# Keys and values of the first cross attention made at the program's start and kept in DRAM

## The chip, the core and the metric

The kernel runs on one of the eight cores of a Trainium2 chip. The core has a TensorE (PE in the profile; its weight loads are PEld), a VectorE (DVE), a ScalarE (ACT), a GpSimd (POOL) and a SyncE (SP), each with its own instruction queue, and 16 DMA engines that move data between DRAM and the on-chip buffer. The metric is the device time of one execution in microseconds (us); smaller is better.

## The reference, cut to what matters

Two stacks of layers work on 256 tokens of 1024 features, one after the other. The first stack modulates its norms with a condition vector; its first mixer starts from a modulated norm of the input x. The second stack has two layers, each with a mixer, a cross attention over a fixed memory, and an MLP. Of the cross attention of its layer l (a summary of the reference, not its text):

```
m  = rmsnorm(memory, lnmem[l])                  # 256 x 1024, depends on an input alone
k  = headwise_rmsnorm(m @ xk[l], xkn[l])        # 4 heads of 256
v  = m @ xv[l]
q  = headwise_rmsnorm(rmsnorm(x, lnx[l]) @ xq[l], xqn[l])
x += softmax(q @ k.T / 16) @ v @ xo[l]
mod = silu(cond) @ Wmod + b                     # shift, scale and gate of the first stack
```

Nothing in k and v depends on the first stack: they need only the memory and the weights xk and xv.

## The kernel before, in words

The hidden state is kept transposed on chip, as `xT` of 128 partitions x 8 x 256. All weights stream from DRAM in blocks of 128x1024 float32 (512 KB), issued on SP's queue by `_dma` (L461) into four buffers `wraw`, up to three blocks ahead. Most blocks are then split into a rounded high part `wh` on ACT (L470) and the rest `wl` on DVE (L471), four buffers, two blocks ahead. A product is three matmuls (high x high, high x low, low x high), so a block takes 24 matmuls of 128x256, or 12 of 128x512. A few blocks are used raw: those of the modulation, and the first of the first mixer (`hy_ba`, the first `hy_qkv`).

The order of the blocks is the order in which the program asks for them (`block`). `together` takes turns between generators, one step each; `piped` keeps some units of a stream in flight; `late` starts a generator some turns later. The Tile framework then orders the instructions on each engine and adds the waits.

The start, in `mix` (L849): a `drain` (L891) runs four things side by side. `mod_part` (L726) takes 8 blocks `mod` on DVE, one multiply-and-sum over the block each (L730). `mod_rows` (L745) takes 8 blocks `modk` on PE into `ps_mr`, copies the rows to `mod_row`, and turns them into columns by `ps_mc`; with them `modT` is made. `steps` loads `xT` and sums its squares (`nsq`, `n_sum`). `spectrum` makes a filter for the second stack (`ps_f`, `ps_h`, `ps_abs`, `ps_rb`, and later its transform `ps_F`, with the constant tables `dftu` and `nyq`). Then `modulated` (L893) makes the first mixer's input `h_w` out of `xT`, the row factors `ps_rs` and `modT`, and the first matmuls of the mixer, `ps_g<-h_w,wraw`, follow. On a timeline these matmuls mark the end of the start.

The first cross attention: at the end of the second stack's first mixer (`mixb`, L1675) `memory` (L2146) loads the memory (`c_mem`, ACT's queue) and makes its scaled high and low parts `c_mh`, `c_ml` and its row sums beside the mixer's out projection (`ps_o`). `cross` (L2164) then takes 8 blocks `xv` (`unit_v`, L2210: `ps_v`, into `c_v`), 8 blocks `xk` (`unit`, L2184: `ps_g<-c_mh`, into `c_k`, with squares `c_sq`, their sums `ps_n`, and the norm factor `rf_f` spread over the partitions by `ps_rs`) and 8 blocks `xq` on the state (`ps_g<-hh`, into `c_q`), four units in flight. The attention (`ps_s<-c_k,c_q`) follows. `row_factor` is a chain of small DVE operations (`rf_u`, `is_i`, `is_a`, `rf_f`); the norm of a whole row has a like chain (`is_v` to `is_i`).

## Time and profile before

| what | value |
|---|---|
| time, median of 3 runs | 3307.97 us (3306.54 to 3317.33) |
| profiled execution, its own time | 3313.57 us |
| its span, first to last instruction | 3311.8 us |
| PE busy | 3239.4 us (98%) |
| DVE busy | 2526.4 us (76%) |
| ACT busy | 1599.8 us (48%) |
| mean granted TensorE clock | 0.992 of full speed |

The profiled execution took 1.8 us beside its span, and stands 5.6 us above the median. Busy is the time in which an engine has an instruction in work; PE's matmuls overlap one another, so the step from one start to the next is shorter than the length of a row.

### The profile page before, as it was taken

Reading aid. Unit: us, or ns where it says so; the run is one execution under the profiler, and the core shown is the slowest. Engines: PE = TensorE matmul, PEld = TensorE weight load, DVE = VectorE, ACT = ScalarE, POOL = GpSimd, SP = SyncE. Lnnn points to the kernel's source line nnn. Section 1 sums busy time; section 2 is a strip of 40 time slices with the busy share of each in tenths; the row PEclk is TensorE's granted clock in tenths of the full one; section 3 lists DMA queues with packets and bytes.
Section 4 is the critical chain, followed back from the end, with each engine's and each line's share of the span. In section 5 each row is a group of like instructions: output and inputs, shape, how many; then the busy total and the mean of one; then the engine's idle time right before and its main releaser. Section 6 shows DMA issues by size and latency. Waiting matters only on the chain.

```text
span 3311.8 us, 58824 instructions
## 1 busy us (share of the span) xinstructions
PE 3239.4 (98%) x23096; PEld 2870.1 (87%) x23096; DVE 2526.4 (76%) x5214; ACT 1599.8 (48%) x2530; POOL 11.3 (0%) x24
## 2 busy tenths in 40 slices
PE   7999999999999999999999999999999999999999
PEld 3889999998777769999898788879999987899998
DVE  6878999967977778999856955877766568767655
ACT  4435444444345545444444355555555454545544
POOL 0000000000000000000000000000000000000000
PEclk9999999999999999999999999999999999999999
DMA  7454555687478435655565466525456653545464
GB/s 250 143 184 139 179 180 172 201 276 255 147 251 278 146 103 154 185 184 159 173 185 174 145 192 189 179 87 156 143 164 197 185 158 98 148 138 179 132 188 140
DMA packets 158094, 574.45 MB, mean 173 GB/s; under 512 B 18346, under 2 KB 20077, under 8 KB 157049
## 3 DMA queue, kind: packets, MB, share of 16 engines
q1 hardware_dynamic: 152400, 551.99, 54.4%
q10 hardware_dynamic: 3816, 13.46, 1.1%
q0 software_dynamic: 1600, 5.24, 0.4%
q8 instruction: 181, 2.97, 0.4%
q14 instruction: 97, 0.79, 0.1%
HBM read 564.34 MB, written 6.29 MB: 172 GB/s over the span
## 4 chain that ended last, share of the span: by engine, by line
PE 60%; issue 33%; DVE 5%; ACT 1%; DMA 1%; POOL 0%; SPq 0%; ACTq 0%; POOLq 0%; DVEq 0%
PE ps_g L508 18%; PE acc L508 16%; PE ps_u L508 10%; PE ps_o L508 3%; PE ps_y L508 3%; PE ps_v L508 2%; DVE wl L471 1%; PE ps_s L508 1%; PE ps_po L508 1%; PE ps_F L508 1%; DVE p L520 1%; PE ps_G L508 1%; PE ps_go L508 1%; DMA wraw<-modk 0%; PE ps_pt L533 0%
## 5 line engine op out<-in xcount | busy, mean ns | idle before, releaser
L470 ACT ACTIVATE wh<-wraw 128x1024 fp32r<-128x1024 f32 x932 | 986.8, 1059 | 979.2 <-PE ps_u L508 358.7
L471 DVE TENSOR_TENSOR wl<-wraw,wh 128x1024 fp32r<-128x1024 f32 x932 | 1134.6, 1220 | 336.9 <-ACT wh L470 334.1
L508 PE MATMUL ps_u<-hh,wh 128*128 128x256 f32 x2048 | 580.3, 283 | 0.0
L508 PE MATMUL ps_u<-hh,wl 128*128 128x256 f32 x2048 | 577.5, 282 | 0.0
L508 PE MATMUL ps_u<-hl,wh 128*128 128x256 f32 x2048 | 575.4, 281 | 0.0
L508 PE MATMUL ps_g<-hh,wh 128*128 128x256 f32 (+1 forms) x1920 | 557.9, 292 | 7.5 <-ACT hh L517 4.0
L508 PE MATMUL ps_g<-hl,wh 128*128 128x256 f32 (+1 forms) x1920 | 547.0, 286 | 1.5 <-DVE hl L529 1.5
L508 PE MATMUL ps_g<-hh,wl 128*128 128x256 f32 (+1 forms) x1920 | 547.1, 286 | 0.0
L508 PEld LDWEIGHTS ps_g<-hh,wh 128*128 128x128 f32 x1920 | 367.1, 192 | 23.6 <-issue 6.0
L508 PEld LDWEIGHTS ps_u<-hl,wh 128*128 128x128 f32 x2048 | 387.0, 189 | 0.2
L508 PEld LDWEIGHTS ps_u<-hh,wl 128*128 128x128 f32 x2048 | 387.0, 189 | 0.0
L508 PEld LDWEIGHTS ps_u<-hh,wh 128*128 128x128 f32 x2048 | 385.9, 188 | 0.2
L508 PEld LDWEIGHTS ps_g<-hl,wh 128*128 128x128 f32 x1920 | 369.0, 193 | 7.5 <-issue 2.4
L508 PEld LDWEIGHTS ps_g<-hh,wl 128*128 128x128 f32 x1920 | 369.2, 193 | 0.9 <-issue 0.7
L508 PE MATMUL acc<-wh,pl 128*128 128x512 f32 x976 | 310.8, 398 | 2.9 <-DVE pl L520 2.8
L508 PE MATMUL acc<-wh,ph 128*128 128x512 f32 x976 | 312.8, 400 | 0.0
L508 PE MATMUL acc<-wl,ph 128*128 128x512 f32 x976 | 310.1, 397 | 0.0
L517 ACT ACTIVATE ph<-A 128x256 fp32r<-128x256 f32 x244 | 101.5, 417 | 323.0 <-PE acc L508 167.3
L508 PEld LDWEIGHTS acc<-wh,pl 128*128 128x128 f32 x976 | 181.9, 188 | 50.1 <-DVE pl L520 8.3
L508 PEld LDWEIGHTS acc<-wl,ph 128*128 128x128 f32 x976 | 183.4, 188 | 43.0
L508 PEld LDWEIGHTS acc<-wh,ph 128*128 128x128 f32 x976 | 181.0, 188 | 41.9 <-issue 1.4
L730 DVE SCALAR_TENSOR_TENSOR wraw<-wraw,cond 128x1024 f32<-128x1024 f32 x88 | 107.2, 1221 | 73.1 <-DMA wraw<-mod 72.8
(570 smaller groups left out, 4841.3 us busy)
## 6 DMA issues: line engine op xcount, KB each, us to landing
wraw<-u SPq DMA_DIRECT2D x256, 512.0 KB
wraw<-v SPq DMA_DIRECT2D x256, 512.0 KB
wraw<-w SPq DMA_DIRECT2D x128, 512.0 KB
wraw<-mod SPq DMA_DIRECT2D x88, 512.0 KB
wraw<-b_gate SPq DMA_DIRECT2D x48, 512.0 KB
wraw<-pq SPq DMA_DIRECT2D x32, 512.0 KB
wraw<-b_hy SPq DMA_DIRECT2D x24, 512.0 KB
wraw<-b_gla SPq DMA_DIRECT2D x18, 512.0 KB
```

The lines of the kernel that those rows point to most:

```text
L470: self.nc.scalar.activation(h, raw, AF.Copy)
L471: self.nc.vector.tensor_tensor(l, raw, h.bitcast(F), op=OP.subtract)
L508: self.nc.tensor.matmul(out, lhsT, rhs, start=start, stop=stop, skip_group_check=skip)
L517: self.nc.scalar.activation(out, in_, func, bias=bias, scale=scale, **k)
L520: self.nc.vector.tensor_tensor(out, a, b, op=op)
L730: self.nc.vector.scalar_tensor_tensor(w, w, 0.5, self.cond, op0=OP.mult, op1=OP.mult, accum_out=self.modT[l][:, j:j + 1])
```

## The change

In `mix`, before the mixer's own buffers are taken, `memory` is now called for the first cross attention. Its norm, the 8 `xv` blocks and the 8 `xk` blocks (`memory_units`, four units in flight) run inside the opening `drain`, taking turns with the modulation's weights; the spectrum starts four turns later. When keys and values are ready they are stored, 1 MB each, by GpSimd's DMA queue into a DRAM buffer `kv`. At the end of `mixb` the two are loaded back on ACT's queue in place of the memory and its norm, and `cross` of the first layer takes only its 8 `xq` blocks before the attention. The second layer's cross attention still makes its keys and values itself, by the same helper, in which `unit_v` now hands on after each block. The buffers of the first mixer are allocated after those of the new work are released.

```diff
             ectx = ExitStack()
             eps_ = ectx.enter_context(tc.tile_pool(name="earlyps", bufs=1, space=PSUM, reuse_waits="tile"))
...
+            def steps():
+                yield
+                for k in range(0, KT, 4):
+                    self.nc.scalar.dma_start(self.xT[:, k:k + 4], self.ap["xT"][:, k:k + 4])
+                yield
...
+            with ExitStack() as before:
+                ahead = iter(())
+                if "cross0" in self.stages:
+                    self.memory(0, before)
+                    (mem, nm), self.mem = self.mem, None
+                    kvp = before.enter_context(tc.tile_pool(name="memkv", bufs=1, reuse_waits="tile"))
+                    k = kvp.tile([P, KT, T], F, name="c_k")
+                    vt = kvp.tile([P, 2, D], F, name="c_v")
+                    self.kv = tc.dram_tile([P, 2, KT, T], F, name="kv")
+
+                    def prepared():
+                        for i in range(2, KT, 2):
+                            nm.step(i)
+                            nm.step(i + 1)
+                            yield
+                        yield from nm.tail()
+
+                    def stored():
+                        nm.step(0)
+                        nm.step(1)
+                        yield from together(prepared(), piped(self.memory_units(0, kvp, mem, nm, k, vt), 4))
+                        self.nc.gpsimd.dma_start(self.kv[:, 0], k)
+                        self.nc.gpsimd.dma_start(self.kv[:, 1], vt.rearrange("p t (a n) -> p (t a) n", n=T))
+
+                    ahead = stored()
+                first = before.enter_context(tc.tile_pool(name="first", bufs=1, reuse_waits="tile"))
+                self.cond_columns(first)
+                next(spectrum, None)
+                drain(together(ahead, self.mod_rows(0, 0, 8, first, eps_), self.mod_part(0, 8, 16), steps(),
+                               late(4, some(6, spectrum))))
             pool = ctx.enter_context(tc.tile_pool(name="hyb", bufs=1, reuse_waits="tile"))
...
-            drain(together(self.mod_part(0, 8, 16), self.mod_rows(0, 0, 8, early, eps_), steps(), some(6, spectrum)))
             self.load_constants()
             self.modulated(nrm, 0, 0, hw)
...
-                prepare = self.memory(l, self.memctx)
+                if l == 0 and self.kv is not None:
+                    kvp = self.memctx.enter_context(tc.tile_pool(name="memkv2", bufs=1, side="right", reuse_waits="tile"))
+                    k = kvp.tile([P, KT, T], F, name="c_k")
+                    vt = kvp.tile([P, 2, D], F, name="c_v")
+                    nc.scalar.dma_start(k, self.kv[:, 0])
+                    nc.scalar.dma_start(vt.rearrange("p t (a n) -> p (t a) n", n=T), self.kv[:, 1])
+                    self.mem = (k, vt, None)
+                else:
+                    prepare = self.memory(l, self.memctx)
             drain(together(self.project_out(f"b_out{l}", mh, ml), prepare))
...
+    def memory_units(self, l, pool, m, nm, k, vt):
+        def unit_v(b):
+            outs = [self.ps.tile([P, 512], F, name="ps_v", tag="mm") for _ in range(2)]
+            for i in range(4):
+                w = self.block(f"xv{l}", b * 4 + i)
+                self.gemm_o1(outs, w, m, 2, 2 * i, i == 0, i == 3)
+                yield
+            while nm.r is None:
+                yield
+            for t in range(2):
+                self.act(vt[:, t, b * 512:(b + 1) * 512], outs[t], AF.Copy, scale=nm.r[:, t:t + 1])
+            yield
+        for b in range(2):
+            yield unit_v(b)
+        for i in range(4):
+            yield self.cross_unit(pool, f"xk{l}", i, m, k, f"xkn{l}", nm)
...
+            def projections():
+                if len(held) == 2:
+                    yield from self.memory_units(l, pool, *held, k, vt)
                 for i in range(4):
-                    yield unit(f"xq{l}", i, (self.hh, self.hl), q, f"xqn{l}", nrm)
+                    yield self.cross_unit(pool, f"xq{l}", i, (self.hh, self.hl), q, f"xqn{l}", nrm, made)
```

Three places show how the instructions stand. First, SP's queue from its first weight block on, before the change; `mod0` and `modk0` are the modulation's blocks for DVE and for PE.

```order
L461 DMA wraw_134<-mod0 128x1024
L461 DMA wraw_136<-modk0 128x1024
L461 DMA wraw_138<-mod0 128x1024
L461 DMA wraw_140<-modk0 128x1024
L461 DMA wraw_142<-mod0 128x1024
L461 DMA wraw_144<-modk0 128x1024
```

The same queue from the same place on, with the change; `xv0` and `xk0` are the blocks of values and keys, `cst` a table of constants.

```order
L461 DMA wraw_150<-xv0 128x1024
L461 DMA wraw_156<-modk0 128x1024
L461 DMA wraw_158<-mod0 128x1024
L461 DMA wraw_160<-xv0 128x1024
L717 DMA cst_70<-cst 128x1668
L461 DMA wraw_162<-xv0 128x1024
L461 DMA wraw_164<-modk0 128x1024
L461 DMA wraw_183<-mod0 128x1024
L461 DMA wraw_191<-xv0 128x1024
L461 DMA wraw_204<-xv0 128x1024
L461 DMA wraw_220<-xk0 128x1024
```

The 16 modulation blocks are now spread among 16 blocks of values and keys, and the constants come earlier.

Second, PE's last instructions ahead of the first mixer, before the change; `ps_mr` and `ps_mc` make the modulation's columns, `ps_rs<-cst,is_i` the row factors of x.

```order
L508 MATMUL ps_mr<-wraw,condc 1x512 x8
L508 MATMUL ps_abs<-cst,f_sum 128x1 x4
L508 MATMUL ps_rb<-cst,f_rn 128x128
L508 MATMUL ps_mc<-one,mod_row 128x1 x4
L508 MATMUL ps_rs<-cst,is_i 128x128 x2
L508 MATMUL ps_rb<-cst,f_rn 128x128 x3
L508 MATMUL ps_g<-h_w,wraw 128x256 x16
```

The same place with the change; `ps_n<-cst,c_sq` and `ps_rs<-cst,rf_f` belong to the norm of the last key heads, `ps_ss<-cst,n_sum_335` to the norm of x, `ps_F` to the spectrum.

```order
L508 MATMUL ps_rs<-cst,rf_f 128x128 x2
L508 MATMUL ps_n<-cst,c_sq 128x1 x2
L508 MATMUL ps_ss<-cst,n_sum_335 128x1 x2
L508 MATMUL ps_abs<-cst,f_sum 128x1 x4
L508 MATMUL ps_rb<-cst,f_rn 128x128 x4
L508 MATMUL ps_rs<-cst,rf_f 128x128 x2
L508 MATMUL ps_mc<-one,mod_row 128x1 x4
L508 MATMUL ps_F<-f_678,nyq 1x512
L508 MATMUL ps_rs<-cst,is_i 128x128 x2
L508 MATMUL ps_F<-f_678,nyq 1x512
L508 MATMUL ps_F<-f_678,dftu_120 128x512 x2
L508 MATMUL ps_g<-h_w,wraw 128x256 x12
```

The norm of the last key heads, the sum of x's norm and a part of the transform `ps_F` now stand between the last modulation block and the first `h_w` matmul.

Third, PE at the end of the second stack's first mixer, before the change; `ps_o` is the out projection.

```order
L508 MATMUL ps_o<-mh,wl 128x256
L508 MATMUL ps_v<-wh,c_mh 128x512
L508 MATMUL ps_v<-wl,c_mh 128x512
L508 MATMUL ps_v<-wh,c_ml 128x512
L508 MATMUL ps_v<-wh,c_mh 128x512
```

The same place with the change; `ps_g<-hh` and `ps_g<-hl` are the queries, made of the state.

```order
L508 MATMUL ps_o<-mh,wl 128x256
L508 MATMUL ps_g<-hh,wh 128x256
L508 MATMUL ps_g<-hl,wh 128x256
L508 MATMUL ps_g<-hh,wl 128x256
L508 MATMUL ps_g<-hh,wh 128x256
```

The queries' matmuls follow the out projection directly; the 16 blocks of values and keys are gone from this place.

## Rows read from the trace of the kernel before

**Rows 1.** The page, part 1 and part 4: PE, and the chain's shares.
```profile
PE 3239.4 (98%) x23096; PEld 2870.1 (87%) x23096; DVE 2526.4 (76%) x5214; ACT 1599.8 (48%) x2530; POOL 11.3 (0%) x24
...
PE 60%; issue 33%; DVE 5%; ACT 1%; DMA 1%; POOL 0%; SPq 0%; ACTq 0%; POOLq 0%; DVEq 0%
```

**Rows 2.** Cross attention by stretches: length, PE, PEld, DVE, ACT, POOL busy, clock, DMA share, GB/s.
```profile
2357.00:2394.84 37.84, 37.84 (x321) 37.65 (x320) 37.34 (x81) 27.63 (x52) 0.00 (x0) 1.00 0.63 185
2394.84:2418.83 23.99, 23.99 (x110) 19.22 (x109) 17.02 (x40) 11.45 (x14) 0.00 (x0) 1.00 0.67 212
2418.83:2447.50 28.67, 28.67 (x243) 28.61 (x242) 18.20 (x48) 15.59 (x25) 0.00 (x0) 1.00 0.59 171
```

**Rows 3.** Timeline there: start, length, engine, line, operation, out<-in, [idle before <-releaser].
```profile
2394.84 0.40 PE L508 MATMUL ps_v<-wh,c_mh 128*128 128x512 f32 x1
...
2396.99 0.48 DVE L529 SCALAR_TENSOR_TENSOR hl<-xT,vec,hh 128x256 fp32r<-128x256 f32 x1
...
2397.18 0.56 PE L508 MATMUL ps_ss<-cst,n_sum 128*128 128x1 f32 x4
...
2404.77 0.71 PE L508 MATMUL ps_rs<-cst,is_i 128*128 128x128 f32 x4
...
2444.35 0.36 PE L508 MATMUL ps_g<-hh,wh 128*128 128x256 f32 x1
...
2445.92 0.15 DVE L520 TENSOR_TENSOR rf_u<-ps_n,n_r 128x2 f32<-128x2 f32 x1
...
2450.12 0.64 PE L508 MATMUL ps_rs<-cst,rf_f 128*128 128x128 f32 x4
```

**Rows 4.** The start by stretches, columns as in Rows 2.
```profile
0.00:13.67 13.67, 1.08 (x3) 0.32 (x3) 3.98 (x12) 3.69 (x6) 0.20 (x4) 1.00 0.79 266
13.67:49.09 35.42, 28.90 (x83) 8.70 (x83) 22.66 (x62) 10.24 (x18) 0.00 (x0) 1.00 0.91 306
0.00:49.09 49.09, 29.98 (x85) 9.02 (x85) 26.64 (x73) 13.92 (x24) 0.20 (x4) 1.00 0.88 295
```

**Rows 5.** Timeline of the start, columns as in Rows 3.
```profile
13.67 3.57 PE L508 MATMUL ps_mr<-wraw,condc 128*1 128x512 f32 x4 [2.22 <-DMA wraw<-modk]
...
27.88 1.88 PE L508 MATMUL ps_mr<-wraw,condc 128*1 128x512 f32 x4 [0.87 <-DMA wraw<-modk]
...
42.42 1.88 PE L508 MATMUL ps_mr<-wraw,condc 128*1 128x512 f32 x4 [0.67 <-DMA wraw<-modk]
...
47.25 0.16 DVE L520 TENSOR_TENSOR modT<-ps_mc,vec 128x4 f32<-128x4 f32 x1 [1.56 <-PE ps_mc L508]
...
49.09 7.93 PE L508 MATMUL ps_g<-h_w,wraw 128*128 128x256 f32 x32 [0.56 <-DVE h_w L524]
...
61.68 1.88 PE L508 MATMUL ps_F<-f,nyq 128*1 128x512 f32 x4
...
63.48 3.70 PE L508 MATMUL ps_F<-f,dftu 128*128 128x512 f32 x8
...
66.15 0.42 ACT L517 ACTIVATE rope_s<-rr_r 128x256 f32<-128x256 f32 x1
```

**Rows 6.** PE by operation from 0 to 49.09: busy, mean ns, idle before.
```profile
L508 PE MATMUL ps_mr<-wraw,condc 128*1 128x512 f32 x32 | 18.9, 722 | 7.5 <-DMA wraw<-modk 7.5
...
L508 PE MATMUL ps_f<-f_z,f_w 33*64 33x256 f32 x2 | 1.1, 640 | 10.4 <-DMA f_w<-hw 10.4
```

**Rows 7.** Waits of SP's queue, 0 to 60: us in total, times, longest.
```profile
SPq L461 <- PE ps_mr L508: 13.9, 7, 3.1
```

**Rows 8.** The page, part 5: the block operations of DVE and ACT.
```profile
L470 ACT ACTIVATE wh<-wraw 128x1024 fp32r<-128x1024 f32 x932 | 986.8, 1059 | 979.2 <-PE ps_u L508 358.7
L471 DVE TENSOR_TENSOR wl<-wraw,wh 128x1024 fp32r<-128x1024 f32 x932 | 1134.6, 1220 | 336.9 <-ACT wh L470 334.1
```

**Rows 9.** DMA issues of POOL: count, KB each, median us from issue to landing.
```profile
spec<-f_S POOLq DMA_DIRECT2D x20, 256.0 KB, 2.5
```

More of the change, by code (lines that the diff above doesn't have):

```diff
@@ L344, in __init__ @@
         self.sum = []
[L345 removed]
+        self.r = self.rs = self.r2 = None
     def squares(self, k):
@@ L853, in mix @@
         with ExitStack() as ctx:
+            ectx = ExitStack()
+            eps_ = ectx.enter_context(tc.tile_pool(name="earlyps", bufs=1, space=PSUM, reuse_waits="tile"))
+            pn_ = eps_.tile([P, 16], F, name="ps_n")
+            pn = [pn_[:, 0:8], pn_[:, 8:16]]
+            spool = ectx.enter_context(tc.tile_pool(name="spectra", bufs=1, side="right", reuse_waits="tile"))
+            spectrum = self.spectra(0, spool, eps_, "sf") if "mixb0" in self.stages else iter(())
+            def steps():
[3 more added lines that the diff above has]
+                yield
+                for k in range(KT):
+                    nrm.step(k)
+                    yield
+                nrm.finish()
@@ L2162, in memory, with cross_unit @@
         return prepare()
+    def cross_unit(self, pool, name, hd, x, dst, wn, nr, made=None):
+        ps = self.ps.tile([P, 2, T], F, name="ps_g", tag="mm")
+        for j in range(2):
+            w = self.block(name, 2 * hd + j)
+            self.gemm_o2(ps[:, j, :], w, x)
+            if made is None:
+                yield
+        yield
+        yield
+        sq = pool.tile([P, 2, T], F, name="c_sq", bufs=2)
+        d = dst[:, 2 * hd:2 * hd + 2, :]
+        self.act(sq, ps, AF.Square)
+        for j in range(2):
+            self.act(d[:, j, :], ps[:, j, :], AF.Copy, scale=self.v(wn, j))
+        self.tt(sq[:, 0, :], sq[:, 0, :], sq[:, 1, :], OP.add)
+        pn = self.ps.tile([P, 2], F, name="ps_n", tag="aux")
+        for t in range(2):
+            self.mm(pn[:, t:t + 1], sq[:, 0, t * P:(t + 1) * P], self.c("ones")[:, 0:1], True, True, True)
+        yield
+        r = self.row_factor(pool, pn[:, :, None], nr, 256, 1.0 if made is None else 1.0 / 16.0)[:, :, 0]
+        if made is not None:
+            made[hd] = r
+            return
+        pb = self.ps.tile([P, 2, P], F, name="ps_rs", tag="aux")
+        for t in range(2):
+            self.spread(pb[:, t, :], r[:, t:t + 1])
+        self.tt(d, d, pb.rearrange("p a b -> p (a b)")[:, None, :].to_broadcast([P, 2, T]), OP.mult)
+    def memory_units(self, l, pool, m, nm, k, vt):
[4 more added lines that the diff above has]
+                self.gemm_o1(outs, w, m, 2, 2 * i, i == 0, i == 3)
+                yield
+            while nm.r is None:
+                yield
+            for t in range(2):
+                self.act(vt[:, t, b * 512:(b + 1) * 512], outs[t], AF.Copy, scale=nm.r[:, t:t + 1])
+            yield
+        for b in range(2):
+            yield unit_v(b)
+        for i in range(4):
+            yield self.cross_unit(pool, f"xk{l}", i, m, k, f"xkn{l}", nm)
     def cross(self, l, nrm):
@@ L2176, in cross @@
             q = pool.tile([P, KT, T], F, name="c_q")
-            k = pool.tile([P, KT, T], F, name="c_k")
-            vt = pool.tile([P, 2, D], F, name="c_v")
+            if len(held) == 3:
+                k, vt = held[:2]
+            else:
+                k = pool.tile([P, KT, T], F, name="c_k")
+                vt = pool.tile([P, 2, D], F, name="c_v")
             oh = pool.tile([P, KT, T], R, name="c_oh")
@@ L2210, in unit_v @@
-            def unit_v(b):
-                outs = [self.ps.tile([P, 512], F, name="ps_v", tag="mm") for _ in range(2)]
-                for i in range(4):
-                    w = self.block(f"xv{l}", b * 4 + i)
-                    self.gemm_o1(outs, w, m, 2, 2 * i, i == 0, i == 3)
-                for t in range(2):
-                    self.act(vt[:, t, b * 512:(b + 1) * 512], outs[t], AF.Copy, scale=nm.r[:, t:t + 1])
-                yield
-            def projections():
-                for b in range(2):
-                    yield unit_v(b)
-                for i in range(4):
-                    yield unit(f"xk{l}", i, m, k, f"xkn{l}", nm)
-                for i in range(4):
-                    yield unit(f"xq{l}", i, (self.hh, self.hl), q, f"xqn{l}", nrm)
+            def projections():
+                if len(held) == 2:
+                    yield from self.memory_units(l, pool, *held, k, vt)
+                for i in range(4):
+                    yield self.cross_unit(pool, f"xq{l}", i, (self.hh, self.hl), q, f"xqn{l}", nrm, made)
```

50 lines of the change are left out of this document (4 added, 46 removed).

## The prediction

> **What bounds the kernel now.** I read the page first: PE is busy 98% of the span, and the chain that ended last is PE for 60% and PE's issue for 33% [rows 1]. So work taken off PE comes off the end only where PE stands still somewhere else, since the moved work has to be done all the same. The question is whether the place it leaves was full and the place it goes to was empty.
>
> The place it leaves was read by stretches. In the out projection and the first cross attention PE is busy 37.84 of 37.84 us, 23.99 of 23.99 and 28.67 of 28.67 at full clock [rows 2]; DVE, ACT and the DMA engines are below that. PE sets the pace there. The reader should see that the first value matmul starts at 2394.84, directly behind the out projection, and the first query matmul at 2444.35 [rows 3].
>
> The place it goes to was read by stretches too: up to the first `h_w` matmul at 49.09 PE is busy for only 29.98 us, while the DMA engines are 88% busy at 295 GB/s [rows 4]. The timeline has the waits at every modulation block on PE, and the end of the start at 49.09 [rows 5]. By operation, PE stood 10.4 us until its first weights landed and 7.5 us for modulation blocks [rows 6]. SP's queue in turn waited 13.9 us in 7 pieces for `ps_mr` to free a buffer [rows 7]. So the start has about 49.1 - 30.0 = 19.1 us of idle PE, 12.6 of it (13.67 - 1.08) before the first modulation block.
>
> **The change part by part.**
>
> *Removed from the cross attention.* From 2394.84 to 2444.35 is 49.5 us. In it stand the sum and the factors of x's own norm, which stay: `ps_ss` at 2397.18 and `ps_rs` at 2404.77, 0.56 and 0.71 long [rows 3], of which about 1.0 in the stream. Behind it stand the last key heads' `ps_rs` and `ps_n`, one of them at 2450.12 at 0.64; three such go too, about 1.6. Gone: 49.5 - 1.0 + 1.6 = 50.1 us of PE that was never waiting.
>
> *Cover lost there.* The last columns of the state's low part `hl` are made at 2396.99 and ready near 2397.5 [rows 3], which the value matmuls hid. Now the queries come directly behind the out projection. A block's 24 matmuls have a step of about 0.117 (28.67 / 243), so its eighth column is reached at about 2394.84 + 21 x 0.117 = 2397.3: a wait of 0.2 to 0.5; I take 0.3. The norm's chain (`rf_u` at 2445.92 up to `ps_rs` at 2450.12, so at most 4.2 us) has four query pairs, some 23 us, to hide in: nothing. Loading keys and values, 2 MB instead of the memory's 1 MB, lies beside the out projection, where the DMA share is 0.63: nothing, and if it landed late, the first query pairs would still cover it. Taking the memory's norm off DVE and ACT in the out projection gains nothing, as PE did not wait there.
>
> *Added at the start, on PE.* The same 50.1 us less the rounding of the seams; I take 49.5, which is the length of the stretch it left. In order of PE, the first transform products `ps_F`, one of 1.88 and about half of the 3.70, now stand ahead of the `h_w` matmuls; that is 3.8 us moved earlier and not added [rows 5].
>
> How late is the first `h_w` matmul? Work of before: 29.98, of which `ps_mr` 18.9 where eight groups at 1.88 make 15.0, so 26.1 at full rate [rows 4 to 6]. All of it with the new work: 26.1 + 49.5 + 3.8 = 79.4. It cannot begin before the first weights, so from 13.67 (less the 1.1 of `ps_f` done by then) it ends at 92.0 if PE never waits again. Two waits are added.
>
> First, the tail. Before, x's factors were ready long before the last modulation group (42.42), and from its end at 44.30 to 49.09 PE had 4.8 us with some 2 idle (`modT` waits 1.56, `h_w` 0.56). Now PE's order has the last heads' `ps_n`, x's `ps_ss`, the heads' `ps_rs`, and x's `ps_rs` behind one another. Two chains of small DVE operations (up to 4.2 us each, as above) stand between them, with about 3 us of other PE work beside them. In PE's strict order everything behind a waiting `ps_rs` waits, `ps_mc` and `h_w` with it. I take 3.5 us idle, bounds 2 to 6.
>
> Second, the buffers in the middle. Both value units are in flight together, and the third to eighth value blocks must each find a free pair of the four split buffers, which PE releases only when it has used the pair before. Behind the waiting split on ACT stand the squares for x's norm. Each split is 1.06 on ACT and 1.22 on DVE [rows 8], a block's matmuls about 2.8. Nothing of this shows in the trace of before; the nearest rows are SP's waits of 13.9 in 7 pieces, about 2 us each [rows 7]. Below, zero; above, seven such waits, 13.9. As part of PE's work goes on from the modulation blocks meanwhile, I take one piece and a bit, 2.5.
>
> So the first `h_w` matmul is expected at 92.0 + 3.5 + 2.5 = 98.0, and the start is longer by 98.0 - 49.1 - 3.8 = 45.1 us.
>
> *DMA and the other engines at the start.* 16 blocks and the memory are 9.4 MB more on the 14.5 MB of before (49.09 us at 295 GB/s), in all 23.9 MB, 81 us at that rate: below 98, so DMA does not set the end, though it is close. DVE has 26.6 + 16 x 1.22 and some 20 of norms, about 66; ACT less. Both lie beside PE.
>
> *The stores.* Keys and values leave on POOL's queue, which before had nothing until the filter's spectrum. 256 KB took 2.5 us to land [rows 9]; 1 MB costs between that and four times as much, 10 us. Four times is the bound that I use: keys ready near 94, landed by about 104. What waits for it is the mixer's rotary table `rope_s` on ACT, whose buffer lies where the keys lay. It stood 17 us behind the first `h_w` matmul (66.15 against 49.09), so about 115 now: nothing. If the store were later, ACT would stand at that row with the splits of the mixer's weights queued behind it, and PE behind these.
>
> *Sum.* -50.1 + 0.3 + 45.1 = -4.7 us against the profiled execution's 3313.57. That execution stands 5.6 above the median, and nothing in the sum depends on that, so I apply it to the median: 3307.97 - 4.7, about 3303.
>
> *A rule weighed.* The first modulation group takes 3.57 us and a later one 1.88 [rows 5]. So PE ran at half rate, 1.2 instead of 2.4 GHz, after having done 1.1 us of work in 13.67, though the granted clock column says 1.00 for that stretch. The Trainium skill, TensorE: Matmul & The Clock Gate, "What's actually happening", says that the throttled clock is the default and that activity releases it. The trace agrees: full rate comes after the first groups. By that rule the denser start would run at full rate sooner, and up to 18.9 - 15.0 = 3.9 us more would be gained, which leads to 3299; by the row alone the first blocks of the new start pay the same, and the sum stands. I leave it out, since whichever block comes first still comes after the same idle time.
>
> **The rivals.**
>
> 1. *The idle time is filled much better.* For it: 19.1 us of idle PE, and the order now has split weights for PE between modulation blocks. With no wait in the middle, a tail of 2 and the half-rate groups gone, `h_w` starts at 90 to 92: 37 to 39 us later net, a gain of 11 to 13, and the filter work done earlier may give some 2 more. Time 3293 to 3297. Against it: 12.6 of the idle time lies before any weights have landed, where no order helps.
>
> 2. *The start starves (slower).* At the third to eighth value block PE stands with both value units open, because the split's buffer, its data or the DVE in front of it is late, and each such stop also delays the raw modulation blocks behind it, in the buffers as in PE's order. The price is two to four us a stop; from about 15 us of stops beyond the 2.5 taken, the loss passes 9.9. With seven stops as in [rows 7], and PE at half rate for a part of it, `h_w` starts near 114: 3319. For it: DMA is already 88% busy, and PE is given more work from one stream of the same four buffers. Against it: 81 us of data and 66 of DVE leave slack before 98.
>
> 3. *Moved, and nothing filled.* Idle time stays 19 us and the tail is added: `h_w` at 49.1 + 49.5 + 3.8 = 102.4, net 49.5 longer: 3308. This lies within the forecast's own range.
>
> 4. *The store or the load is late.* The rotary table waits, or the first attention does. The price is some 5 to 10 us, and it decides from a store landing after 115. I give it little, as its bound of 104 is 11 us clear.
>
> **How the numbers follow.** 0.3% of 3308 is 9.9 us, about what a measurement of this kernel can tell from no change: faster is below 3298, slower above 3318. Forecast with rival 3: 0.56, all within 0.3%, its own range 3298 to 3311. Rival 1: 0.26. Rivals 2 and 4 together: 0.18, of which 4 is 0.03. The range reaches from 3291, which leaves out the last part of rival 1, to 3319, the middle of rival 2.
>
> **What would show it.** Right: the first query matmul directly behind the last `ps_o` with a gap below 1 us; the stretch before it gone by 49 to 51 us; the first `h_w` matmul between 95 and 102; PE's idle time in the start 15 to 20 us, most of it before 14 and in the last 10 us. Wrong: `h_w` before 93 (rival 1), or after 110 with PE's waits named on `ps_v` for splits or data (rival 2); `rope_s` waiting for the store; or the first `ps_s` waiting for `c_k`.

## The result: slower by about 22 us

| | before | after |
|---|---|---|
| median of 5 runs | 3307.97 us (3306.54 to 3317.33) | 3330.03 us (3325.76 to 3336.6) |
| profiled execution | 3313.57 us | 3336.6 us |
| its span | 3311.8 us | 3334.8 us |
| mean granted TensorE clock | 0.992 | 0.988 |

Both medians are of five runs; the table ahead of the prediction says three for before, with the same median and range. The ratio is 1.0064, with an interval of [1.0048, 1.008]. So the kernel after is slower by 0.64%, a small loss that is clear of the scatter of the runs. The forecast was 3303, a small gain inside 0.3%; its range ended at 3319. The prediction was wrong.

The page of the kernel after, the same two lines as [rows 1]:

```profile
PE 3254.9 (98%) x23096; PEld 2879.3 (86%) x23096; DVE 2527.9 (76%) x5214; ACT 1597.7 (48%) x2528; POOL 12.4 (0%) x26
...
PE 59%; issue 34%; DVE 4%; ACT 1%; DMA 1%; POOL 0%; SPq 0%; ACTq 0%; POOLq 0%; DVEq 0%
```

PE has the same 23096 instructions and is busy 15.5 us longer (3254.9 against 3239.4). The work is the same and takes more time.

To see where, I set each instruction of DVE and ACT beside the same one of before, and took the median of how much later it runs. The table follows this shift along the program; `ps_u` are matmuls of the first stack's mixer.

| stretch of the kernel after | shift at its end | change |
|---|---|---|
| the start and the rest of the first mixer's opening, to the first `ps_u` (275.8) | +57.6 | +57.6 |
| from there to the end of the second stack's first mixer (2457) | +62.2 | +4.6 |
| first cross attention | +13.2 | -49.0 |
| to 3015 | +16.5 | +3.3 |
| second cross attention | +24.0 | +7.5 |
| end of the span | +23.0 | -1.0 |

Two of these steps stand beside half rate, the lower of TensorE's two clock levels: the shift is already +63.6 at 380, behind 17 us of half rate (1.2 of 2.4 GHz) between 293 and 317, and the +3.3 comes at 2963 to 2969, where the clock is 0.50.

**What came as forecast.** In the first cross attention the queries follow the out projection without a gap. The timeline of after there (start, length, engine, line, operation, out<-in):

```profile
2457.79 0.28 PE L508 MATMUL ps_o<-mh,wl 128*128 128x256 f32 x1
2457.90 0.28 PE L508 MATMUL ps_g<-hh,wh 128*128 128x256 f32 x1
```

The step is 0.11 us, where [rows 3] had 49.5 us of values, keys and norms. The stores landed early. The DMA issues of after, KB each, and median us to landing; behind them the mixer's rotary table:

```profile
kv<-c_v POOLq DMA_DIRECT2D x1, 1024.0 KB, 5.2
kv<-c_k POOLq DMA_DIRECT2D x1, 1024.0 KB, 4.1
```
```profile
106.73 0.54 POOL L892 DMA_DIRECT2D kv<-c_k  x1 [45.03 <-DVE c_k L520]
...
125.07 0.42 ACT L517 ACTIVATE rope_s<-rr_r 128x256 f32<-128x256 f32 x1
```

The keys' store was issued at 106.73 and landed near 111, some 14 us before `rope_s`, which shows no wait in front of it. The fourth rival is out. The first `ps_s` (2482.72) shows no wait for `c_k` either. The bound of 10 us for 1 MB (four times [rows 9]) was far too high. The Trainium skill, DMA: Bandwidth & Descriptors, "Anatomy of one DMA", gives 2.0 us and the bytes at 436 GB/s for a DMA of GpSimd's queue; for 1 MB that is an estimate of 4.4. The measured 4.1 and 5.2 lie on either side of it.

**What did not: the start.** Stretches of the kernel after (length, busy time and instructions of PE, PEld, DVE, ACT, POOL, granted clock, DMA share, GB/s), which answer to [rows 4]:

```profile
10.00:20.00 10.00, 8.21 (x21) 3.62 (x22) 9.48 (x22) 7.32 (x17) 0.00 (x0) 1.00 0.98 373
20.00:30.00 10.00, 6.33 (x25) 3.26 (x23) 7.39 (x24) 3.34 (x6) 0.00 (x0) 1.00 1.00 396
30.00:40.00 10.00, 7.35 (x19) 3.76 (x19) 7.88 (x16) 6.90 (x11) 0.00 (x0) 0.83 0.90 289
40.00:50.00 10.00, 10.00 (x35) 7.48 (x36) 4.26 (x7) 4.43 (x6) 0.00 (x0) 0.83 0.47 151
...
90.00:100.00 10.00, 8.83 (x39) 4.92 (x38) 6.69 (x39) 2.71 (x4) 0.00 (x0) 0.94 0.63 185
98.80:112.40 13.60, 10.20 (x29) 6.05 (x30) 9.39 (x29) 0.56 (x2) 0.54 (x1) 0.50 0.19 77
```

From 10 to 30 the DMA engines are full. Between 23 and 40 PE waits six times, 6.3 us in all, mostly for splits; the two longest:

```profile
27.25 0.73 PE L508 MATMUL ps_v<-wh,c_mh 128*128 128x512 f32 x2 [1.22 <-ACT wh L470]
38.65 0.73 PE L508 MATMUL ps_v<-wh,c_mh 128*128 128x512 f32 x2 [1.84 <-ACT wh L470]
```

Behind these waits the clock is at half, 1.2 GHz, for 3.4 us from 30.5 and again from 40.8, although PE is then busy without a stop. From 50 to 90 PE runs without a stop at 1.00. At 98.8, among short matmuls and waits of 0.2 to 0.5 us, the clock falls to half again and stays there to 112.5; PE's longest stand, 3.40 us, comes after this fall and not before it. PE's timeline there (the last column is idle time and what ended it), which answers to the last modulation group and the `h_w` row of [rows 5]:

```profile
95.44 0.50 PE L508 MATMUL ps_n<-cst,c_sq 128*128 128x1 f32 x4
...
98.77 2.08 PE L508 MATMUL ps_rb<-cst,f_rn 128*128 128x128 f32 x8 [0.48 <-DVE is_a L520]
104.25 1.20 PE L508 MATMUL ps_rs<-cst,rf_f 128*128 128x128 f32 x4 [3.40 <-DVE rf_f L529]
105.38 1.86 PE L508 MATMUL ps_mc<-one,mod_row 1*128 1x1 f32 x8
107.17 1.86 PE L508 MATMUL ps_F<-f,nyq 128*1 128x512 f32 x2
108.97 1.22 PE L508 MATMUL ps_rs<-cst,is_i 128*128 128x128 f32 x4
...
113.98 0.81 PE L508 MATMUL ps_g<-h_w,wraw 128*128 128x256 f32 x3
```

The first `h_w` matmul is at 113.98, forecast 98.0. The sum of the last keys is ready at 95.9, and the factor made of it is used at 104.25. All that stands behind that `ps_rs` in PE's order waits, and runs at half rate: two `ps_F` matmuls take 1.86, where four took 1.88 in [rows 5]. DVE's timeline says why the factor is late:

```profile
96.31 0.15 DVE L520 TENSOR_TENSOR rf_u<-ps_n,n_r 128x2 f32<-128x2 f32 x1
...
100.89 1.22 DVE L520 TENSOR_TENSOR f<-f,ps_rb 128x1024 f32<-128x1024 f32 x1 [0.88 <-PE ps_rb L508]
...
102.17 1.22 DVE L520 TENSOR_TENSOR f<-f,ps_rb 128x1024 f32<-128x1024 f32 x1
...
103.97 0.14 DVE L529 SCALAR_TENSOR_TENSOR rf_f<-is_i 128x2 f32<-128x2 f32 x1
```

The chain `rf_u` to `rf_f` takes 7.7 us, against at most 4.2 in [rows 3]. In DVE's order it is mixed with the chain of x's norm and with two operations of the filter, 1.22 each, of which the first waits for PE's `ps_rb`.

**And the second cross attention.** Its values, keys and queries are the same work in both kernels, but its helper now hands on after each block. The stretch of its value matmuls, of before, and then of after:

```profile
3002.30:3026.60 24.30, 23.99 (x110) 19.06 (x109) 17.57 (x41) 11.22 (x14) 0.00 (x0) 1.00 0.68 213
```
```profile
3019.60:3050.20 30.60, 26.84 (x114) 19.78 (x112) 17.07 (x39) 11.99 (x15) 0.00 (x0) 0.96 0.56 185
```

It is 6.3 us longer. PE stands for 3.8 us of it, against 0.3 before, and about 1.1 more is half rate at its end (3047.9 to 3050.2). PE's longest waits of after in it:

```profile
3029.50 0.71 PE L508 MATMUL ps_rs<-cst,is_i 128*128 128x128 f32 x4 [0.86 <-DVE is_i L529]
3038.32 1.08 PE L508 MATMUL ps_v<-wh,c_mh 128*128 128x512 f32 x2 [1.14 <-ACT wh L470]
3045.68 0.73 PE L508 MATMUL ps_v<-wh,c_mh 128*128 128x512 f32 x2 [1.15 <-ACT wh L470]
```
```profile
3037.22 1.06 ACT L470 ACTIVATE wh<-wraw 128x1024 fp32r<-128x1024 f32 x1 [2.88 <-PE ps_v L508]
```

PE waits for a split on ACT, and ACT had waited 2.88 us for PE to free a split's buffer. Before, one unit was finished and then the other, and PE waited for no split there: its only wait is 0.31 for x's norm. The likely reason is that with both value units in work by turns the four pairs of split buffers are held by the two units together, so that the next split can't run ahead. That the turns are the cause is shown below (e1, e2); that it is by the buffers is argued from these rows.

### The profile page after: what moved, and what is told of

Same layout as the page of the kernel before. It is cut to its first block, busy times and chain, and to the rows that moved or that the text cites. A ratio compares the mean times of both kernels' runs of the same rounds, so it can differ in the third digit from the quotient of the medians.

```text
span 3334.8 us, 58831 instructions
## 1 busy us (share of the span) xinstructions
PE 3254.9 (98%) x23096; PEld 2879.3 (86%) x23096; DVE 2527.9 (76%) x5214; ACT 1597.7 (48%) x2528; POOL 12.4 (0%) x26
## 4 chain that ended last, share of the span: by engine, by line
PE 59%; issue 34%; DVE 4%; ACT 1%; DMA 1%; POOL 0%; SPq 0%; ACTq 0%; POOLq 0%; DVEq 0%
PE ps_g L508 17%; PE acc L508 16%; PE ps_u L508 10%; PE ps_o L508 3%; PE ps_y L508 3%; PE ps_v L508 2%; PE ps_s L508 1%; DVE wl L471 1%; PE ps_F L508 1%; PE ps_po L508 1%; PE ps_go L508 1%; DVE p L520 1%; PE ps_G L508 1%; ACT wh L470 1%; PE ps_pt L533 0%
## 5 line engine op out<-in xcount | busy, mean ns | idle before, releaser
L471 DVE TENSOR_TENSOR wl<-wraw,wh 128x1024 fp32r<-128x1024 f32 x932 | 1135.9, 1221 | 358.2 <-ACT wh L470 355.6
L508 PE MATMUL ps_u<-hh,wh 128*128 128x256 f32 x2048 | 580.2, 283 | 0.0
L508 PE MATMUL ps_u<-hh,wl 128*128 128x256 f32 x2048 | 577.4, 282 | 0.0
L508 PE MATMUL ps_u<-hl,wh 128*128 128x256 f32 x2048 | 575.3, 281 | 0.0
L508 PE MATMUL ps_g<-hh,wh 128*128 128x256 f32 (+1 forms) x1920 | 556.8, 292 | 9.6 <-ACT hh L517 4.3
L508 PE MATMUL ps_g<-hl,wh 128*128 128x256 f32 (+1 forms) x1920 | 545.1, 285 | 1.2 <-DVE hl L529 1.2
L508 PE MATMUL ps_g<-hh,wl 128*128 128x256 f32 (+1 forms) x1920 | 545.0, 285 | 0.0
L508 PEld LDWEIGHTS ps_g<-hh,wh 128*128 128x128 f32 x1920 | 365.5, 191 | 26.5 <-issue 6.0
L508 PEld LDWEIGHTS ps_u<-hl,wh 128*128 128x128 f32 x2048 | 386.9, 189 | 0.2
L508 PEld LDWEIGHTS ps_u<-hh,wl 128*128 128x128 f32 x2048 | 387.0, 189 | 0.0
L508 PEld LDWEIGHTS ps_u<-hh,wh 128*128 128x128 f32 x2048 | 385.8, 188 | 0.2
L508 PEld LDWEIGHTS ps_g<-hl,wh 128*128 128x128 f32 x1920 | 366.8, 191 | 8.0 <-issue 2.7
L508 PEld LDWEIGHTS ps_g<-hh,wl 128*128 128x128 f32 x1920 | 367.0, 192 | 0.9 <-issue 0.7
L508 PE MATMUL acc<-wh,ph 128*128 128x512 f32 x976 | 312.8, 400 | 0.0
L508 PE MATMUL acc<-wh,pl 128*128 128x512 f32 x976 | 310.1, 397 | 1.2 <-DVE pl L520 1.1
L508 PE MATMUL acc<-wl,ph 128*128 128x512 f32 x976 | 310.1, 397 | 0.0
L508 PEld LDWEIGHTS acc<-wh,pl 128*128 128x128 f32 x976 | 182.4, 188 | 46.3 <-DVE pl L520 3.9
L508 PEld LDWEIGHTS acc<-wl,ph 128*128 128x128 f32 x976 | 183.3, 188 | 43.1
L508 PEld LDWEIGHTS acc<-wh,ph 128*128 128x128 f32 x976 | 180.9, 188 | 41.9 <-issue 1.4
```

What stands on the lines that cost most here:

```text
L471: self.nc.vector.tensor_tensor(l, raw, h.bitcast(F), op=OP.subtract)
L508: self.nc.tensor.matmul(out, lhsT, rhs, start=start, stop=stop, skip_group_check=skip)
```

## Experiments

The kernels below were timed beside the kernel before, whose median was then 3308.5 to 3309.9. "Idle", "lost to half rate" and "work" are PE's, from the trace, up to the first `ps_u` matmul. Idle is counted from PE's first matmul at about 10 us on; lost is half of PE's busy time where the clock is recorded at 0.50; work is the rest of its busy time. Before: work 190.2, idle 14.3, lost 3.4. After: 239.3, 17.8 and 8.5. So of the 57.6 us about 49.1 are the moved work, 3.5 more idle time and 5.1 more half rate: the start took in the work and filled none of its idle time with it.

**Where the loss is: four parts, each alone**

*The second cross attention put back (e1).* The new turns are taken only at the start:

```diff
                 self.gemm_o1(outs, w, m, 2, 2 * i, i == 0, i == 3)
-                yield
+                if turns:
+                    yield
```

> The changed kernel, but in the second layer's cross attention the value and key units take their blocks in the order of before (no turn handed on after each block); the start keeps its turns. Theory A, the helper's new turns cost the second cross attention about 7 to 10 us: 3320 to 3323 us, and the second cross attention's value matmuls take about 24.3 us again instead of 30.6. Theory B, the step of some 10 us that the two traces show between 2950 and 3050 us is a chance fall of the clock: 3330 us.

3322.78 us (3319.52 to 3327.47), ratio 1.005 [1.0037, 1.0064]; that is 7.3 below after, as theory A had it. Its value matmuls there are back at 23.8 us at full clock. The start is as slow as in after (first `h_w` at 113.05).

*The turns alone (e2)*, in both cross attentions of the kernel before:

```diff
                     self.gemm_o1(outs, w, m, 2, 2 * i, i == 0, i == 3)
+                    yield
```

> The kernel before, with nothing but the new turns of the value and key units, in both cross attentions. Theory A: each cross attention loses 7 to 10 us, so 3322 to 3328 us. Theory B: 3308 us.

3319.65 (3317.22 to 3324.65), ratio 1.0038 [1.0024, 1.0052]: about 11 us for two cross attentions, less than the 14 to 20 that theory A had for them, and far from theory B's nothing. In its trace the shift at the end is 10.5: about 7 and 6 are added in the two, and it runs 3 ahead of before where the first begins. So the helper's new turns cost in either place, where nothing else takes turns with it.

*The start alone (e3).* Keys and values are made and stored at the start and not used:

```diff
-                if l == 0 and self.kv is not None:
+                if False:
```

> Keys and values are made at the start and stored, but never used: the first cross attention makes its own as before, and both cross attentions have the order of before. Theory A, the start costs what the traces show as its shift, about 60 to 61 us: 3368 us. Theory B, the start costs only the 49 to 51 us that were taken out of the cross attention and the rest arises later: 3358 us.

3370.41 (3367.35 to 3375.21), ratio 1.0192 [1.0176, 1.0208]. The start costs 61.9 us, for about 49 us of work.

*The first cross attention alone (e4).* The start of before; keys and values are loaded from an input:

```diff
-                prepare = self.memory(l, self.memctx)
+                if l == 0:
...
+                    nc.scalar.dma_start(k, self.ap["memT"])
```

> Start of before; the first cross attention loads its keys and values at the end of the mixer from the memory itself, so the projections of keys and values and the memory's norm are left out in that layer and what it attends to is other data; both cross attentions in the order of before. Both theories: the removal is worth 50 us, 3258 us. Under 45 us of gain would mean that loads or lost cover hold up the queries.

3258.38 (3256.88 to 3259.9), ratio 0.9853 [0.9838, 0.9868]: 50.2 us less. The parts add up to within 3 us: 61.9 - 50.2 + 7.3 = 19.0, measured 22.

**Why the start is dear.** Theories: the new work's order leaves waits that another order fills (order); the data of the blocks comes late (data); the last norm's chain is lengthened by the filter on DVE (filter); the keys' norms, wherever they stand, add latency that PE can't fill (key norms). All from here on have the old order in the second cross attention.

*The filter held back (e9)* until `h_w` is made:

```diff
             self.modulated(nrm, 0, 0, hw)
+            with tc.issue_after(self.last):
+                next(spectrum, None)
```

> The kernel of the first experiment (new start, old order in the second cross attention; 3322.8 us, first h_w matmul at 112.6), with one thing more: the filter's long DVE operations (each 1.2 us) are held on DVE behind the last operation that makes the first mixer's input, so that they no longer stand inside the last key heads' norm chain, and the filter's transform no longer stands ahead of the h_w matmuls on PE. Theory A, the tail of the start is that chain and PE's half rate behind it: first h_w matmul at 101 to 104, and 3314 to 3317 us (the transform's 3.8 us come back later). Theory B, the start is bound by PE's work and by data, and the tail only shows it: 3320 to 3323 us.

3317.51 (3310.53 to 3323.84), ratio 1.0022 [1.0012, 1.0032], 5.3 below e1. PE's timeline:

```profile
96.88 1.59 PE L508 MATMUL ps_abs<-cst,f_sum 128*128 128x1 f32 x8 [0.19 <-DVE f_sum L520]
99.28 1.19 PE L508 MATMUL ps_rs<-cst,rf_f 128*128 128x128 f32 x4 [0.81 <-DVE cv_x L966]
100.40 1.86 PE L508 MATMUL ps_mc<-one,mod_row 1*128 1x1 f32 x8
102.19 1.23 PE L508 MATMUL ps_rs<-cst,is_i 128*128 128x128 f32 x4
104.65 1.65 PE L508 MATMUL ps_g<-h_w,wraw 128*128 128x256 f32 x3 [1.23 <-DVE h_w L524]
```

The wait for `rf_f` is down from 3.41 in e1 to 0.81, and `h_w` starts at 104.65, 8.4 earlier than in e1. But the matmuls are still at half rate (`ps_mc` 1.86). By the first `ps_u` nothing of the 8 us is left in this trace (275.6 against 274.6): 10.6 us are lost to half rate against 8.2, and the filter's work is still to be done. So theory A comes close (`h_w` at 101 to 104, 3314 to 3317 us). But the profiled execution took 3323.84, 6.3 above the median, so where the medians' gain lies isn't traced.

*Modulation first, keys and values every second turn (e7)*; then the same with the filter held (e10):

```diff
-                drain(together(ahead, self.mod_rows(0, 0, 8, first, eps_), self.mod_part(0, 8, 16), steps(),
-                               late(4, some(6, spectrum))))
+                drain(together(self.mod_rows(0, 0, 8, first, eps_), self.mod_part(0, 8, 16), steps(),
+                               some(6, spectrum), every(2, ahead)))
```

> The kernel of the first experiment, but in the opening round the modulation, x's norm and the filter come ahead of keys and values, which take a step only every second turn, so that x's sum and the modulation's last blocks are done before the last key heads. Theory A: nothing but the last key heads' norm stands behind the last key matmul, first h_w matmul at 100 to 105, 3312 to 3316 us. Theory B: 3320 to 3323 us.

> Both changes of the two experiments above together. Theory A: the tail has little left to lose, first h_w matmul at 97 to 101, 3308 to 3313 us. Theory B: 3320 to 3323 us.

3318.42 (3312.18 to 3330.02), ratio 1.0033 [1.0022, 1.0044], and 3325.27 (3321.98 to 3328.2), ratio 1.005 [1.0037, 1.0063]. The first lies between the ranges of its two theories, the second above both. In the first the half rate moved from the tail to the middle (17 us from 35 on) and cost 11.9; its `h_w` comes only at 122.88, as late keys and the filter stand ahead of it. In the second the keys stand last, `h_w` is at 114.16, and PE waits 3.17 and 2.71 in front of the factors of two heads one after the other. Neither idles less than before's 14.3 (16.8 and 21.6).

*As e10, without turns inside the units, memory norm first (e12):*

```diff
-                        yield from together(prepared(), piped(self.memory_units(0, kvp, mem, nm, k, vt, True), 4))
+                        yield from together(nm.tail(), piped(self.memory_units(0, kvp, mem, nm, k, vt), 4))
```

> The kernel of the experiment with both changes, and the value and key units take their blocks without a turn after each, with the memory's norm steps all first. Theory A with the waits in the middle counted (6.3 us of idle PE between 23 and 40, and about 3.4 us lost to half rate there): first h_w matmul at 93 to 98, 3303 to 3309 us, level with before or a little better. Theory B, the middle waits come from the split buffers and stay: 3308 to 3313 us.

3323.08 (3318.54 to 3324.31), ratio 1.0036 [1.0024, 1.0049]; idle 20.2. No gain over e1, and above the ranges of both theories.

*Without the blocks' data (e15).* The 16 blocks are filled on the chip instead of loaded:

```diff
+        if name in ("xv0", "xk0"):
+            self.nc.gpsimd.memset(t, 0.015625)
+        else:
+            self.nc.sync.dma_start(t, self.ap[name][j])
```

> The kernel of the first experiment (3322.8 us), but the 16 blocks of keys and values at the start are not loaded: GpSimd sets them to a constant, so 8.4 MB of data are left out there and the first cross attention gets other keys and values. Theory D, PE's waits between 12 and 40 us come from the data, since the DMA engines are 90 to 100% busy until then: those waits (some 6 us) and the two half-rate stretches behind them shrink, 3314 to 3319 us. Theory O, they come from the order on PE and from the split buffers: 3320 to 3324 us, with the same waits for the splits.

3325.76 (3317.64 to 3328.48), ratio 1.0047 [1.0035, 1.0059]. Its stretches, the columns as above:

```profile
0.00:20.00 20.00, 9.35 (x27) 4.56 (x28) 11.34 (x23) 11.96 (x21) 4.97 (x9) 1.00 0.71 259
20.00:40.00 20.00, 16.79 (x51) 8.91 (x50) 14.88 (x36) 8.82 (x17) 5.16 (x6) 0.83 0.55 187
40.00:60.00 20.00, 17.60 (x77) 13.84 (x77) 12.57 (x20) 7.97 (x12) 4.93 (x6) 0.83 0.26 80
```

The DMA share falls to 0.55 and 0.26, and the time is no shorter: it is a little above theory O's range. PE's waits between 12 and 60 are 6.4 us in e1 and 5.9 here, now all of one kind (L511 and L474 are L508 and L471 of the other kernels):

```profile
PE ps_v L511 <- DVE wl L474: 5.9, 3, 3.0
```

The data was late in e1: there ACT waited 10.4 us for value blocks before it could split them. With that wait gone, PE waits as long for the low part of the split on DVE. So the data theory falls as the reason for the loss: earlier data alone does not shorten the start. (The fill takes POOL about 15 us here; ACT waited 1.3 us for it between 12 and 60.)

*Keys and values first, modulation last (e18)*, six turns late and with the filter held, and the same without turns inside the units (e19):

```diff
+                drain(together(ahead, late(6, self.mod_rows(0, 0, 8, first, eps_)), late(6, self.mod_part(0, 8, 16)),
+                               steps(), late(8, some(6, spectrum))))
```

> The first experiment's kernel with the filter's long operations held behind h_w (3317.5 us), and keys and values first in the opening round: the modulation starts six turns later, the filter eight. Theory D: blocks with 2.8 us of PE work each come ahead of the modulation's, whose DVE half brings PE none, so PE waits less between 12 and 40 us, and the tail is the modulation's own: first h_w matmul at 95 to 99, 3308 to 3313 us. Theory O: 3316 to 3321 us.

> As the one above, but the value and key units take their blocks without a turn after each, all steps of the memory's norm come first, and the modulation starts two turns later and the filter four. Theory D: 3308 to 3313 us. Theory O: the value units no longer hold two pairs of split buffers open at a time, so fewer waits for the splits, 3310 to 3315 us.

3319.47 (3317.09 to 3323.05), ratio 1.0031 [1.002, 1.0042], and 3324.61 (3322.56 to 3327.48), ratio 1.0045 [1.0032, 1.0058]. The first lies in theory O's range, the second above both. The first ends its keys at 74.7, 30 us before `h_w` (104.7), and PE waits for no key's factor in the tail; it is no better than e9. The second idles 21.4. Of these orders none idles less than before's start did: the order theory falls too, as far as these orders go.

*Values only (e21).* The keys stay in the first cross attention; then the same with the values behind the modulation (e23), and e21 with the filter held (e26):

```diff
-            yield unit_v(b)
-        for i in range(4):
+            yield unit_v(b)
+        for i in range(4 if "k" in what else 0):
```

> The first experiment's kernel (new start, old order in the second cross attention; +13 to +14 us), but only the 8 value blocks are made at the start and kept in DRAM; the first cross attention makes its keys itself, and no key norm stands in the start. 24 us of PE work move instead of 50. Theory T, the loss is a fixed one, made by the last key heads' norm chain and the half rate in the start's tail: without key norms the tail is that of before, 3305 to 3311 us, first h_w matmul at 72 to 75. Theory P, the loss goes with the work that is moved (waits between the blocks, and half rate after them): half of it, 3314 to 3317 us, first h_w matmul at 77 to 82.

> As the one above, with the modulation, x's norm and the filter ahead of the values in each turn. Theory T: as above or up to 3 us less, 3303 to 3310 us. Theory P: 3314 to 3317 us.

> Values alone at the start (3312.4 us, 2.9 above before), with the filter's long operations held behind h_w on DVE. In the profile of values alone the tail has one wait of 2.2 us, for x's own factors. Theory T: the rest of the loss is that tail, 3306 to 3310 us, level with before. Theory P: 3311 to 3314 us, since holding the filter only moves its work.

e21: 3312.41 (3310.61 to 3325.85), ratio 1.0013 [1.0003, 1.0023], the best of the kernels that do all the work. The end of its start, PE's timeline:

```profile
68.34 1.05 PE L508 MATMUL ps_mc<-one,mod_row 1*128 1x1 f32 x8
71.57 0.68 PE L508 MATMUL ps_rs<-cst,is_i 128*128 128x128 f32 x4 [2.19 <-DVE is_i L529]
72.09 1.35 PE L508 MATMUL ps_abs<-cst,f_sum 128*128 128x1 f32 x8
73.48 2.93 PE L508 MATMUL ps_g<-h_w,wraw 128*128 128x256 f32 x6
```

Theory T has its `h_w` right (73.48), and the time lies between the two theories. `ps_mc` runs at full rate, and the one wait left in the tail is x's own norm. Idle is 13.4, less than before; half rate costs 6.8. It moves half the work and gets back about what it costs, no more: 23.6 us later behind the start, 22.6 given back in the first cross attention. e23: 3317.51 (3311.09 to 3322.95), ratio 1.0024 [1.0015, 1.0033]; a wait of 4.67 for a modulation block at 50.1, and theory P's time. e26: 3323.1 (3320.43 to 3330.99), ratio 1.0043 [1.0028, 1.0057]. That is worse by 10.7 than e21, where holding the filter had helped e9. Its PE timeline behind the start:

```profile
98.92 1.98 PE L508 MATMUL ps_F<-f,dftu 128*128 128x512 f32 x4 [0.94 <-ACT f_S L517]
...
111.75 1.01 PE L508 MATMUL ps_n<-cst,cv_q 128*128 128x1 f32 x4 [2.60 <-ACT cv_q L517]
```

The filter that was held now stands inside the mixer's opening, and PE waits there: idle 18.7 against 13.4, lost to half rate 12.2 against 6.8, together about the 10.7. Both theories had missed this.

*No norm for the keys at the start (e24).* e1, with its squares, sums and factors left out:

```diff
-        self.act(sq, ps, AF.Square)
+        if not turns:
+            self.act(sq, ps, AF.Square)
...
+        if turns:
+            return
```

> The first experiment's kernel (all 16 blocks at the start, old order in the second cross attention; 3322.8 us), but the heads' norm of the keys made at the start is left out: no squares, no ps_n, no factor chain, no ps_rs, no multiplication, so the first cross attention gets unnormalised keys. That takes 4.6 us of PE's time out (1.8 of ps_n and 2.8 of ps_rs, partly at half rate). Theory T, the key norms' chains make the fixed loss of the start: far more than that is gained, 3308 to 3312 us, first h_w matmul at 98 to 101. Theory P, only their PE work and nothing else: 3317 to 3320 us, first h_w matmul at 107 to 109.

3309.26 (3300.44 to 3312.84), ratio 0.9995 [0.9985, 1.0005]: 13.5 below e1, for 4.8 us of PE work left out (235.4 against 240.2). That is theory T's time. ACT and DVE lose the norms' work as well. Its tail:

```profile
94.31 1.05 PE L508 MATMUL ps_mc<-one,mod_row 1*128 1x1 f32 x8
96.87 1.86 PE L508 MATMUL ps_abs<-cst,f_sum 128*128 128x1 f32 x8 [1.52 <-DVE f_sum L520]
99.20 1.22 PE L508 MATMUL ps_rb<-cst,f_rn 128*128 128x128 f32 x4 [0.47 <-DVE is_a L520]
100.22 1.06 PE L508 MATMUL ps_rs<-cst,is_i 128*128 128x128 f32 x4
101.07 1.06 PE L508 MATMUL ps_rb<-cst,f_rn 128*128 128x128 f32 x4
102.51 7.93 PE L508 MATMUL ps_g<-h_w,wraw 128*128 128x256 f32 x32 [0.38 <-DVE h_w L524]
```

`h_w` starts 10.5 earlier than in e1. The clock falls here too, but for 6.8 us instead of 13.7. Set against e1 the shift is -7.6 by the first `ps_u` and -13.3 by 450; the last 5 or so come in the first stack's mixer, where this trace has 6.8 us of half rate between 280 and 360 and e1's has 20.4 in the stretch that answers to it. So the key norms are shown to cost the start some 7.6 us with their work. That they also bring the later 5 is not shown: e3, with the start of e1 and all its key norms, has 6.8 us of half rate from 10 to 50 us behind its first `ps_u`, where e1 has 17.1 and before 6.8.

## Why the prediction was wrong

- **What bounds the kernel** (PE, so that moved work comes off only where PE stood idle): right. But none of the idle time was filled: up to the first `ps_u` it is 17.8 us after and 14.3 before.
- **Removed from the cross attention, 50.1 less 0.3:** right. Alone it measures 50.2; in after's own trace 49.0.
- **Stores, loads, rotary table, nothing:** right.
- **The start, +45.1: this step failed.** `h_w` is at 113.98, not 98.0, and alone the start costs 61.9. The failing sentence is that all of the work, 79.4, ends at 92.0 "if PE never waits again", since the 79.4 was summed at full rate. PE is busy for 91.3 up to `h_w`. Of the 11.9 more, 8.5 is the half rate from 30.5, from 40.8 and from 98.8 on, as far as PE had work in it, and 1.7 the slow first modulation group (16.7 for the eight, against 15.0); the last 1.7 is not placed. Its tail, "3.5 us idle, bounds 2 to 6", measures 4.6 (0.51, 0.19, 0.48 and 3.40), near enough; the half rate there was not priced, and cost 5.1, more than the waits. Its middle, 2.5, measures 6.3 in six waits (the modulation block at 23.62 with 1.14, splits at 27.25, 30.28, 38.65 and 39.91, `is_i` at 29.14), with 3.4 of half rate behind them. Why the clock falls in these places is not shown. In the tail it falls ahead of the 3.40 us wait, and e9 has the same 13.7 us of half rate with 0.81 in its place, so that wait is not the reason.
- **The second cross attention: a term that is missing.** The front of this document says that its helper hands on after each block; the sum has no line for it. It measures +7.3.
- **A rule weighed.** The prediction named up to 3.9 us more gain from a start that comes to full rate sooner. But its sum had these 3.9 already, since it set the eight modulation groups at 15.0 instead of 18.9; its 3299 counts them twice, and so does rival 1's `h_w` at 90 to 92, where the sum's own 92.0 and a tail of 2 give 94.0. Of the 3.9, 2.2 came in (16.7 against 18.9). The loss stands against it: 0.83 from 30 to 50 and 0.50 from 98.8 to 112.4, where the stretches of before are at 1.00 up to 60. The start was denser in the mean and not in its tail. The rule was that of the Trainium skill (TensorE: Matmul & The Clock Gate, "What's actually happening"), that the throttled clock is the default and activity releases it.

Put together: 12.5 more in the start to the first `ps_u` (57.6 against 45.1), 4.6 from there to the first cross attention, 0.8 less given back, 7.5 in the second cross attention and 2.3 of smaller shifts are the 27.7 between -4.7 and the +23.0 of the two spans.

**The rivals.** By its time rival 2 (slower) is the nearest. Its 114 for `h_w`, its "half rate for a part of it" and the waits for splits are there; but its place is half wrong. It put the stops in the middle; there 6.3 us are idle and 3.4 lost to half rate, and in the tail, where no block is waited for, as much again, 4.6 and 5.1. Its 114 was summed from seven stops for buffers, so that this number was met is in part luck. By PE's idle time rival 3 (nothing filled) is the nearest: the 19.1 us stayed and the tail came on top, 22.7 measured up to `h_w`. Its 102.4 leaves out the tail that it names; with 3.5 for it `h_w` would stand at 105.9, and the 8.1 from there to 113.98 is about the size of the half rate (8.5). None of the rivals knew of the second cross attention.

**What stays open.** Why the same stretch of the first stack's mixer runs longer at half rate in after: windows of before, then of after, in the same part of it.

```profile
234.00:241.00 7.00, 7.00 (x27) 5.23 (x27) 1.46 (x4) 1.15 (x4) 0.00 (x0) 0.52 0.00 0
241.00:262.00 21.00, 21.00 (x156) 19.05 (x156) 11.45 (x31) 7.22 (x15) 0.00 (x0) 1.00 0.17 43
```
```profile
293.00:300.00 7.00, 7.00 (x27) 5.28 (x28) 1.47 (x4) 1.48 (x5) 0.00 (x0) 0.53 0.00 1
300.00:317.00 17.00, 17.00 (x83) 14.61 (x82) 5.00 (x15) 3.08 (x10) 0.00 (x0) 0.70 0.01 1
```

The clock comes back at 241 in the one and not for good until about 317 in the other. Such stretches may differ from run to run of one kernel as well: after's five runs have mean clocks of 0.988 to 0.993 and spans of 3334.8 to 3324.0. And the traces with all 16 blocks at the start have from 6.8 us of half rate there (e3, e7, e10, e12) to 17.1 (after, e1, e9). So 5 us of it can't be put down to the change. Also open: why the clock falls at 98.8, which part of the keys' norm costs most, and why values behind the modulation (e23) are no better than between it.

## What to carry to other kernels

Before work is moved into an engine's idle time, follow the last piece of it to its consumer: its closing chain of small operations comes to stand in the engine's strict order ahead of what already waited there, and behind whatever shares the other engine. Freeing that one chain is not the whole price, though: it gave back 5 of 62 us here (e9). Price the moved work at the rate of the place it goes to, not of the place it came from: in the cross attention the work ran at 1.00 throughout, and the start with it has 20.5 us at half rate. And when a shared helper is changed for one caller, read the order at its other callers too; here that alone cost a third of the loss.

## What the hardware showed that was not expected

- The granted clock was 0.50 from 98.8 to 112.4 while PE was busy 10.20 of 13.6 us, and 0.53 from 293 to 300 while it was busy 7.00 of 7.00. A busy PE in the profile is not a PE at full clock.
- Once down, it stayed so through dense work: from 104.25 to 112 PE has no wait, and its `ps_F` matmuls of 512 columns at 107.17 and 110.12 still take twice their time (1.86 for two).
- Ending the wait did not end the half rate: with the 3.40 cut to 0.81 (e9) the stretch still lasted 13.7 us.
